# A gated DeltaNet layer on one core: inverse substitution in place, two batches in turns, a third vt buffer

## The chip, the cores and the metric

The kernel runs on one core of a Trainium2 chip. The metric is the device time of one execution, in microseconds. Engines are named as the profile names them: PE (matrix multiplications, with PEld for its weight loads), DVE (vector), ACT (activation), POOL and SP. SP computes nothing here; it issues most DMA transfers, and ACT and POOL issue the others.

## The reference

The reference is one layer of a diffusion backbone over 1024 latent tokens and 256 context tokens, with 1024 channels. A combined projection feeds two groups of four heads each: a gated DeltaNet that runs over the sequence in both directions, and a retention with rotary positions. Both are followed by norms and gates, one output projection, a SwiGLU and a final norm. What matters here is the gated DeltaNet, which inverts a unit triangular matrix for each chunk, head and direction:

```python
A = jnp.where(strict, jnp.einsum('nbhid,nbhjd->nbhij', kb, kc) * decay, 0.0)
rhs = jnp.concatenate([vc * bc[..., None], kb * jnp.exp(G)[..., None]], axis=-1)
sol = lax.linalg.triangular_solve(A + jnp.eye(CHUNK, dtype=A.dtype), rhs,
                                  left_side=True, lower=True, unit_diagonal=True)
```

The inverse does not depend on the state that the scan carries, so all chunks can be inverted before the scan over the chunks starts.

## The kernel before

The kernel works on ten chunks of 128 tokens, the first two of them context. For each chunk, head and direction there is one 128×128 triangular matrix, 80 in all. They are treated in three batches, `BATCH=[[0,1,2,9],[3,8,4,7],[5,6]]`, in the order in which the two scans need them: 32, 32 and 16 matrices.

**pre(t)** makes the matrices of a chunk. PE multiplies keys with keys into `kk` (line 705) and keys with queries into `kq` (line 715). SP loads a row of gate sums, broadcast, into `gw` (718); POOL masks it into `e` (722); ACT takes exponentials (726); DVE multiplies into `ut` (730) and `sp` (732). SP writes `ut` to `un` in DRAM, one tensor a batch (733), and `sp` into the scan's store `sd` (737).

**invert(b)** inverts the four 32×32 diagonal blocks of each matrix of a batch, one block a partition, so that batches 0 and 1 use 128 partitions and batch 2 uses 64. Four DMAs gather the blocks from `un` in DRAM into `yr` (751). The blocks of one direction are copied by ACT into `L` (758); those of the other are turned on the way by DVE (759). POOL sets `X` to the identity (755, 756). Then there are 31 steps of forward substitution, each a product on DVE (765) and a subtraction (767) that depends on it; the next step depends on that. A turned copy `XT` is made (769), and both are written to `xd` in DRAM (771).

**blocks(b)** and **merge(b)** make the 128×128 inverses from the blocks. SP loads the whole batch from `un` into `U` (783; 2 MB for batches 0 and 1), the diagonal blocks from `xd` over U's diagonal (787), and others into `t64` (788). PE then works in two levels: first `m` from `t64` and `U` (807), a negated copy `xt1` on DVE (810), and products of `xt1` with `U` (814, 817); then the same on blocks of 64 (830, `xt2` at 831, 834). The result goes to `sd`.

**The values.** For each of four heads `conv_block` projects and convolves the value head, with PE at lines 611 to 613, eight DVE operations at line 621 (in segments) and the SiLU on ACT at 624. PE turns the result into `vT` (856), in a PSUM bank that ACT empties into `vt` (859), and ACT issues the write to `sd` (860). `vt` has two buffers.

**token-major** matmuls `tm` (371 to 373) of the gates and the retention projections fill PE's time around the merges; there are 1248 in this phase. Their weights are split by ACT into `whi` (344) and by DVE or POOL into `wlo` (345). Afterwards the scan's steps load `pk` (664) and run `Tr`, `kS`, `up` and others (906 on).

The order of instructions on each engine isn't written out by hand. The program's text gives the dependences and the priorities, and a scheduler with a timeline of its own lays all instructions of the program out. A change in one place so moves instructions in other places too. Each engine, and each DMA queue behind an issuing engine, then runs its row in order: an instruction that waits holds up what stands behind it.

Of the kernel before, what the change touches and what calls it, by code (L numbers as in the profile page):

```python
# [8 lines left out]
F32 = mybir.dt.float32  # L9
F32R = mybir.dt.float32r  # L10
I32 = mybir.dt.int32
AF = mybir.ActivationFunctionType
# [13 lines left out]
H = 4  # L26
# [12 lines left out]
def build(nc, tc, ap, dbg=None, stop=None, marks=None):  # L39
# [151 lines left out]
    try:  # L191
# [508 lines left out]
        def pre(t):  # L700
# [15 lines left out]
            for d in range(2):  # L716
# [13 lines left out]
                V.tensor_tensor(ut.rearrange("p h i -> p (h i)"), pk, e.rearrange("p h i -> p (h i)"), ALU.mult)  # L730
# [12 lines left out]
        def invert(b):  # L743

            nc_ = len(BATCH[b])
            nu = nc_ * H
            nb = 4 * nu
            xd = xds[b] = dr.tile([4 * nb, 1024], F32, tag="xd%d" % b, name="xd%d" % b)
            yr = GI.tile([P, 1024], F32, tag="yr", name="yr", bufs=1)
            for k in range(4):  # L750
                SY.dma_start(yr[k:2 * nb:4].rearrange("r (i j) -> r i j", j=32),
                             un[b][q32[k]].rearrange("i e u j -> (e u) i j")[:, :, q32[k]])
            L = GI.tile([P, 1024], F32, tag="L", name="L", bufs=3)
            X = GI.tile([P, 1024], F32, tag="X", name="X", bufs=2)
            G.memset(X, 0.0)
            G.memset(X[:, 0::33], 1.0)
            m = lambda t: t[:2 * nb].rearrange("p (i j) -> p i j", j=32)
            S.activation(L[:nb], yr[:nb], AF.Copy)
            V.tensor_copy(m(L)[nb:], yr[nb:2 * nb].rearrange("p (i j) -> p j i", j=32))
            for j in range(31):  # L760
                n = 31 - j
                tmp = GI.tile([P, 256], F32, tag="tmp%d" % b, name="tmp", bufs=2)
                t3 = tmp[:2 * nb, :n * (j + 1)].rearrange("p (i c) -> p i c", c=j + 1)
                sh = [2 * nb, n, j + 1]
                V.tensor_tensor(t3, bc(m(L)[:, j + 1:, j], sh, 2), bc(m(X)[:, j, :j + 1], sh, 1), ALU.mult)
                xs = m(X)[:, j + 1:, :j + 1]
                V.tensor_tensor(xs, xs, t3, ALU.subtract)
            XT = GI.tile([P, 1024], F32, tag="L", name="XT", bufs=3)
            V.tensor_copy(m(XT), X[:2 * nb].rearrange("p (i j) -> p j i", j=32))
            for i, x in enumerate((X[:nb], XT[nb:2 * nb], X[nb:2 * nb], XT[:nb])):  # L770
                SY.dma_start(xd[i * nb:(i + 1) * nb], x)
# [20 lines left out]
        def merge(b):  # L792
# [17 lines left out]
            V.tensor_scalar(xt1.rearrange("p n j -> p (n j)")[:, :nu * 32], ps1[:, :nu * 32], -1.0, None, ALU.mult)  # L810
# [14 lines left out]
            for n0 in range(0, nu, 8):  # L825
# [5 lines left out]
                V.tensor_scalar(xt2.rearrange("p n j -> p (n j)"), ps1, -1.0, None, ALU.mult)  # L831
# [9 lines left out]
        def solve(b):  # L841
            for t in BATCH[b]:
                pre(t)
            checkpoint("pre%d" % b)
            invert(b)
            checkpoint("inv%d" % b)

        solve(0)
        solve(1)
        for h in range(H):  # L850
            y = newy()
            conv_block(8 + h, y, False)
            for t0, n in ((0, 2), (2, 4), (6, 4)):
                ps = bank_a("vT")
                for t in range(t0, t0 + n):
                    T.transpose(ps[:, (t - t0) * P:(t - t0 + 1) * P], y[:, t * P:(t + 1) * P], ident)
                vt = CV.tile([P, 4, P], F32, tag="vt", name="vt", bufs=2)
                for t in range(n):
                    S.activation(vt[:, t], ps[:, t * P:(t + 1) * P], AF.Copy, scale=sv3[:, t0 + t, h:h + 1])  # L859
                S.dma_start(vd[t0:t0 + n, :, h, :].rearrange("t p j -> p t j"), vt[:, :n])  # L860
# [12 lines left out]
        invert(2)  # L873
# [781 lines left out]
```

## Time and profile before

| | us |
|---|---|
| median of 3 runs | 1481.14 |
| lowest, highest | 1479.71, 1481.17 |
| the profiled execution's own time | 1477.96 |
| its span, first to last instruction | 1476.2 |
| PE busy in the span | 1397.2 |
| DVE busy | 964.6 |
| ACT busy | 614.0 |
| POOL busy | 590.3 |

The mean granted PE clock was 0.983. The profiled execution is one of its own; its times are read from the first instruction on. In the rows of a timeline stand start, length, engine, line, operation, and what it writes and reads; in square brackets the idle time of the engine before it and what ended that. PEq, SPq and the like are the sequencers that issue.

### The profile page before, as it was taken

The page shows a single profiled execution, that of the slowest core. Times are in us where ns is not written, and L with a number is a line of the kernel's source. Part 1 is how long each engine was busy: PE and PEld are TensorE (multiplying, and loading weights), DVE is VectorE, ACT ScalarE, POOL GpSimd, SP SyncE. Part 2 cuts the span into 40 slices and gives each one's busy share as a digit, 9 for nine tenths or more (in the row PEclk, how much of TensorE's full clock was granted, in tenths as well). Part 3 has the DMA queues.
Part 4 walks back from the last instruction along what each step waited for, and adds up shares of the span by engine and source line. Part 5 has one row for each costly group of instructions (what it writes and reads, how often), then busy time and mean ns, then how long its engine had stood idle before and what let it go on. Part 6 is the DMA issues. An engine that isn't in the chain of part 4 may idle for free.

```text
span 1476.2 us, 24111 instructions
## 1 busy us (share of the span) xinstructions
PE 1397.2 (95%) x8919; PEld 1199.2 (81%) x8919; DVE 964.6 (65%) x1856; ACT 614.0 (42%) x1326; POOL 590.3 (40%) x501
## 2 busy tenths in 40 slices
PE   7999999986789999899799899999999999999997
PEld 2898888975689999898688688877888888788885
DVE  6566789289792435689676877556555564657477
ACT  5643564587333111245443623233333332444445
POOL 0120010243202344234144688898555552335321
PEclk9999999998899999999899999999999999999999
DMA  9536686688888625996532265674222242776863
GB/s 337 197 105 205 189 249 200 219 264 277 282 216 277 238 76 178 416 341 209 184 125 104 97 238 210 242 264 162 105 97 105 107 151 79 260 260 194 288 216 114
DMA packets 170421, 298.14 MB, mean 202 GB/s; under 512 B 43496, under 2 KB 93880, under 8 KB 165952
## 3 DMA queue, kind: packets, MB, share of 16 engines
q1 hardware_dynamic: 118752, 253.17, 50.2%
q10 hardware_dynamic: 49072, 35.83, 7.8%
q0 software_dynamic: 2480, 7.60, 1.4%
q8 instruction: 70, 1.15, 0.3%
q14 instruction: 47, 0.39, 0.1%
HBM read 206.60 MB, written 89.96 MB: 201 GB/s over the span
## 4 chain that ended last, share of the span: by engine, by line
PE 55%; POOL 6%; DMA 5%; DVE 4%; issue 2%; ACT 2%; SPq 1%; ACTq 0%; POOLq 0%; DVEq 0%
PE ffn L1344 7%; PE ffn L1342 6%; PE ffn L1343 6%; PE fo L1470 4%; PE fo L1469 4%; PE fo L1468 4%; PE tm L371 3%; PE tm L373 3%; PE tm L372 3%; PE op L1203 2%; PE op L1201 2%; PE op L1202 2%; DMA wd<-tw 2%; POOL ws L1315 1%; DMA pk<-sd 1%
## 5 line engine op out<-in xcount | busy, mean ns | idle before, releaser
L371 PE MATMUL tm<-whi,hhi 128*128 128x256 f32 (+1 forms) x704 | 199.5, 287 | 7.7 <-ACT vt L859 3.4
L372 PE MATMUL tm<-wlo,hhi 128*128 128x256 f32 (+1 forms) x704 | 199.3, 285 | 2.4 <-issue 2.0
L373 PE MATMUL tm<-whi,hlo 128*128 128x256 f32 (+1 forms) x704 | 197.7, 285 | 0.0
L371 PEld LDWEIGHTS tm<-whi,hhi 128*128 128x128 f32 x704 | 132.8, 190 | 11.8 <-ACT vt L859 3.6
L1342 PE MATMUL ffn<-t,whi 128*128 128x512 f32 x352 | 136.9, 390 | 1.3 <-ACT whi L344 1.3
L1344 PE MATMUL ffn<-t,wlo 128*128 128x512 f32 x352 | 137.0, 390 | 1.0 <-DVE wlo L345 1.0
L1343 PE MATMUL ffn<-t,whi 128*128 128x512 f32 x352 | 137.0, 389 | 0.0
L372 PEld LDWEIGHTS tm<-wlo,hhi 128*128 128x128 f32 x704 | 133.7, 190 | 2.1 <-issue 0.9
L373 PEld LDWEIGHTS tm<-whi,hlo 128*128 128x128 f32 x704 | 132.8, 190 | 2.6 <-issue 1.8
L344 ACT ACTIVATE whi<-wraw 128x512 fp32r<-128x512 f32 (+2 forms) x98 | 75.1, 771 | 141.4 <-PE ffn L1343 80.5
L344 ACT ACTIVATE whi<-ws 128x512 fp32r<-128x512 f32 x88 | 55.6, 632 | 171.5 <-PE ffn L1343 123.4
L345 DVE TENSOR_TENSOR wlo<-ws,whi 128x512 fp32r<-128x512 f32 x88 | 93.9, 1068 | 47.0 <-ACT whi L344 46.8
L1469 PE MATMUL fo<-wlo,ahi 128*128 128x512 f32 x308 | 120.2, 390 | 2.1 <-DVE wlo L345 2.1
L1468 PE MATMUL fo<-whi,ahi 128*128 128x512 f32 x308 | 119.3, 390 | 0.7 <-ACT ahi L344 0.7
L1470 PE MATMUL fo<-whi,alo 128*128 128x512 f32 x308 | 119.0, 390 | 0.0
L345 DVE TENSOR_TENSOR wlo<-wraw,whi 128x512 fp32r<-128x512 f32 (+2 forms) x92 | 99.4, 1082 | 24.6 <-ACT whi L344 24.6
L1342 PE MATMUL ffn<-b,whi 128*128 128x512 f32 x264 | 103.8, 393 | 4.4 <-ACT whi L344 4.4
L1344 PE MATMUL ffn<-b,wlo 128*128 128x512 f32 x264 | 103.6, 393 | 0.8 <-DVE wlo L345 0.8
L1343 PE MATMUL ffn<-b,whi 128*128 128x512 f32 x264 | 103.4, 392 | 0.0
L612 PE MATMUL b<-hlo,whi 128*128 128x512 f32 (+1 forms) x256 | 94.4, 369 | 0.0
L613 PE MATMUL b<-hhi,wlo 128*128 128x512 f32 (+1 forms) x256 | 94.3, 368 | 0.0
L611 PE MATMUL b<-hhi,whi 128*128 128x512 f32 (+1 forms) x256 | 94.3, 368 | 0.0
(446 smaller groups left out, 3448.1 us busy)
## 6 DMA issues: line engine op xcount, KB each, us to landing
adaw<-ada SPq DMA_DIRECT2D x48, 512.0 KB, 4.4
pk<-sd SPq DMA_DIRECT2D x16, 1536.0 KB, 10.0
wraw<-wfi SPq DMA_DIRECT2D x44, 512.0 KB, 3.7
ar<-ad SPq DMA_DIRECT2D x33, 512.0 KB, 4.7
w<-wfo SPq DMA_DIRECT2D x22, 512.0 KB, 5.7
wd<-tw SPq DMA_DIRECT2D x11, 1024.0 KB, 4.8
ad<-act SPq DMA_DIRECT2D x20, 512.0 KB, 3.0
raw<-wd SPq DMA_DIRECT2D x20, 512.0 KB, 4.9
```

Source lines behind the costliest of these rows:

```text
L344: S.activation(hi, raw, AF.Copy)
L345: e.tensor_tensor(lo, raw, hi.bitcast(F32), ALU.subtract)
L371: T.matmul(o, hhi[:, k, tsl], whi[:, k % 4, :], start=(k == 0), stop=False)
L372: T.matmul(o, hhi[:, k, tsl], wlo[:, k % 4, :], start=False, stop=False)
L373: T.matmul(o, hlo[:, k, tsl], whi[:, k % 4, :], start=False, stop=(k == KT - 1))
L612: T.matmul(o, whi[:, k, :], hl, start=False, stop=False)
L1342: T.matmul(o, whi[:, k, :], xhi(xn, slice(0, 4), k), start=(first and k == 0), stop=False, **kw)
L1343: T.matmul(o, whi[:, k, :], xlo(xn, slice(0, 4), k), start=False, stop=False, **kw)
L1344: T.matmul(o, wlo[:, k, :], xhi(xn, slice(0, 4), k), start=False, stop=(k == 3), **kw)
L1468: T.matmul(po[g][i], ahi[:, ts], whi, start=(j == 0 and not kw), stop=False, **kw)
L1469: T.matmul(po[g][i], ahi[:, ts], wlo, start=False, stop=False, **kw)
L1470: T.matmul(po[g][i], alo[:, ts], whi, start=False, stop=(j == FH - 1), **kw)
```

## The change

`ut` is written negated. `invert` takes several batches at once. The blocks of the direction that need not be turned are gathered directly into `X`; the others go into `yr` (now two buffers) and are turned by DVE into `X`. There is no `L` any more, no POOL memset and no ACT copy: `X` starts as the negated matrix, its diagonal is set to one by a small DVE memset, and the steps replace its columns in place. Step 0 falls away, a step works on `j` columns rather than `j + 1`, and subtractions become additions. Where two batches are given, a step writes both products, then both additions. The four gathers of a batch become eight of half the size. `XT` takes its buffers from `X`'s tag. `xt1` and `xt2` become plain copies, and `vt` gets a third buffer.

The order of calls changes as well: `invert(0)` stands alone behind the first batch's `pre`, and `invert(1, 2)` stands behind `merge(0)` where `invert(2)` stood.

```diff
-                V.tensor_tensor(ut.rearrange("p h i -> p (h i)"), pk, e.rearrange("p h i -> p (h i)"), ALU.mult)
+                V.scalar_tensor_tensor(ut.rearrange("p h i -> p (h i)"), pk, -1.0, e.rearrange("p h i -> p (h i)"),
+                                       ALU.mult, ALU.mult)
...
-            for k in range(4):
-                SY.dma_start(yr[k:2 * nb:4].rearrange("r (i j) -> r i j", j=32),
-                             un[b][q32[k]].rearrange("i e u j -> (e u) i j")[:, :, q32[k]])
-            L = GI.tile([P, 1024], F32, tag="L", name="L", bufs=3)
-            X = GI.tile([P, 1024], F32, tag="X", name="X", bufs=2)
-            G.memset(X, 0.0)
-            G.memset(X[:, 0::33], 1.0)
-            m = lambda t: t[:2 * nb].rearrange("p (i j) -> p i j", j=32)
-            S.activation(L[:nb], yr[:nb], AF.Copy)
-            V.tensor_copy(m(L)[nb:], yr[nb:2 * nb].rearrange("p (i j) -> p j i", j=32))
-            for j in range(31):
+        def invert(*bs):
+
+            steps = []
+            for b in bs:
+                nb = 4 * len(BATCH[b]) * H
+                yr = GI.tile([P, 1024], F32, tag="yr", name="yr", bufs=2)
+                X = GI.tile([P, 1024], F32, tag="X", name="X", bufs=4)
+                for e, to in enumerate((X, yr)):
+                    for k in range(4):
+                        SY.dma_start(to[e * nb + k:(e + 1) * nb:4].rearrange("r (i j) -> r i j", j=32),
+                                     un[b][q32[k], e].rearrange("i u j -> u i j")[:, :, q32[k]])
+                m = lambda t, n=2 * nb: t[:n].rearrange("p (i j) -> p i j", j=32)
+                V.tensor_copy(m(X)[nb:], yr[nb:2 * nb].rearrange("p (i j) -> p j i", j=32))
+                V.memset(X[:2 * nb, 0::33], 1.0)
+                steps.append((b, nb, X, m))
+            for j in range(1, 31):
                 n = 31 - j
...
-                V.tensor_tensor(t3, bc(m(L)[:, j + 1:, j], sh, 2), bc(m(X)[:, j, :j + 1], sh, 1), ALU.mult)
-                xs = m(X)[:, j + 1:, :j + 1]
-                V.tensor_tensor(xs, xs, t3, ALU.subtract)
-            XT = GI.tile([P, 1024], F32, tag="L", name="XT", bufs=3)
...
+                for b, nb, X, m in steps:
...
+                    V.tensor_tensor(t3, bc(m(X)[:, j + 1:, j], sh, 2), bc(m(X)[:, j, :j], sh, 1), ALU.mult)
+                    part.append(t3)
+                for (b, nb, X, m), t3 in zip(steps, part):
+                    xs = m(X)[:, j + 1:, :j]
+                    V.tensor_tensor(xs, xs, t3, ALU.add)
...
-        solve(0)
-        solve(1)
+        for t in BATCH[0]:
+            pre(t)
+        invert(0)
+        for t in BATCH[1]:
+            pre(t)
...
-                vt = CV.tile([P, 4, P], F32, tag="vt", name="vt", bufs=2)
+                vt = CV.tile([P, 4, P], F32, tag="vt", name="vt", bufs=3)
...
-        invert(2)
+        invert(1, 2)
```

The layout moves instructions at two places of which the prediction speaks. The first is SP's row of DMA issues around merge 0. `X_4327` is batch 1's matrix in the kernel after, `X_4339` batch 2's; `yr_4440` is batch 2's gather before; `xd0` holds the inverted blocks of batch 0, `U0` and `t64_4177` or `t64_4064` are the tiles of merge 0, and `U1` is that of merge 1. Before:

```order
L783 DMA U1_4550<-un1_2893 128x4096
L771 DMA xd0_3079<-X_3086 64x1024 x2
L771 DMA xd0_3079<-XT_3184 64x1024 x2
L751 DMA yr_4440<-un2_2894 16x32x32 x3
L783 DMA U0_4175<-un0_2892 128x4096
L872 DMA rope_4049<-rope 128x1280
L751 DMA yr_4440<-un2_2894 16x32x32
L788 DMA t64_4177<-xd0_3079 32x32x32 x4
L787 DMA U0_4175<-xd0_3079 32x32x32 x4
```

Now:

```order
L776 DMA xd0_3181<-XT_3182 64x1024
L753 DMA X_4327<-un1_2893 16x32x32 x3
L788 DMA U0_4062<-un0_2892 128x4096
L873 DMA rope_3936<-rope 128x1280
L753 DMA X_4327<-un1_2893 16x32x32
L753 DMA X_4339<-un2_2894 8x32x32
L793 DMA t64_4064<-xd0_3181 32x32x32 x4
L753 DMA X_4339<-un2_2894 8x32x32 x3
L788 DMA U1_4544<-un1_2893 128x4096
L792 DMA U0_4062<-xd0_3181 32x32x32 x4
L776 DMA xd1_4530<-X_4327 64x1024 x2
```

U1's 2 MB load moved from ahead of inverse 0's writes to a place between merge 0's `t64` loads and its loads of U0's diagonal blocks, and batch 1's last direct gather stands behind U0's 2 MB.

The second place is DVE's row in the middle of inverses 1 and 2, where `tmp` is a product and `X<-X,tmp` the operation that depends on it; operations of 128 partitions belong to batch 1, those of 64 to batch 2. Before, batch 1 alone:

```order
L765 TENSOR_TENSOR tmp<-L,X 128x252
L767 TENSOR_TENSOR X<-X,tmp 128x18x14
L765 TENSOR_TENSOR tmp<-L,X 128x255
L767 TENSOR_TENSOR X<-X,tmp 128x17x15
L765 TENSOR_TENSOR tmp<-L,X 128x256
L767 TENSOR_TENSOR X<-X,tmp 128x16x16
```

Now, the two batches:

```order
L766 TENSOR_TENSOR tmp<-X 128x238
L766 TENSOR_TENSOR tmp<-X 64x184
L770 TENSOR_TENSOR X<-X,tmp 128x17x14
L770 TENSOR_TENSOR X<-X,tmp 64x23x8
L766 TENSOR_TENSOR tmp<-X 128x240
L766 TENSOR_TENSOR tmp<-X 64x198
L770 TENSOR_TENSOR X<-X,tmp 128x16x15
L770 TENSOR_TENSOR X<-X,tmp 64x22x9
```

An addition now has an operation of the other batch between itself and its product. Batch 2 lags seven steps behind and finishes alone.

More of the change, by code (lines that the diff above doesn't have):

```diff
@@ new lines, in invert @@
+        def invert(*bs):
[13 more added lines that the diff above has]
+            for j in range(1, 31):
+                n = 31 - j
+                part = []
+                for b, nb, X, m in steps:
+                    tmp = GI.tile([P, 240], F32, tag="tmp%d" % max(b, 1), name="tmp", bufs=2)
+                    t3 = tmp[:2 * nb, :n * j].rearrange("p (i c) -> p i c", c=j)
+                    sh = [2 * nb, n, j]
+                    V.tensor_tensor(t3, bc(m(X)[:, j + 1:, j], sh, 2), bc(m(X)[:, j, :j], sh, 1), ALU.mult)
[3 more added lines that the diff above has]
+                    V.tensor_tensor(xs, xs, t3, ALU.add)
+            for b, nb, X, m in steps:
+                xd = xds[b] = dr.tile([4 * nb, 1024], F32, tag="xd%d" % b, name="xd%d" % b)
+                XT = GI.tile([P, 1024], F32, tag="X", name="XT", bufs=4)
+                V.tensor_copy(m(XT), X[:2 * nb].rearrange("p (i j) -> p j i", j=32))
+                for i, x in enumerate((X[:nb], XT[nb:2 * nb], X[nb:2 * nb], XT[:nb])):
+                    SY.dma_start(xd[i * nb:(i + 1) * nb], x)
@@ L809, in merge @@
             xt1 = GM.tile([P, 16, 32], F32, tag="xt1", name="xt1", bufs=1)
-            V.tensor_scalar(xt1.rearrange("p n j -> p (n j)")[:, :nu * 32], ps1[:, :nu * 32], -1.0, None, ALU.mult)
+            V.tensor_copy(xt1.rearrange("p n j -> p (n j)")[:, :nu * 32], ps1[:, :nu * 32])
             ps2, ps3 = bank_b("m1"), bank_b("m1")
@@ L830, in merge @@
                         T.matmul(ps1[B, n * 64:n * 64 + 64], u[d][A, n0 + n, B], t[d][A, n0 + n, :], start=True, stop=True)
-                V.tensor_scalar(xt2.rearrange("p n j -> p (n j)"), ps1, -1.0, None, ALU.mult)
+                V.tensor_copy(xt2.rearrange("p n j -> p (n j)"), ps1)
                 for n in range(8):
@@ L839, in merge @@
             checkpoint("mrg%d" % b)
[L841 to L846, printed above, removed]
-        solve(0)
-        solve(1)
+        for t in BATCH[0]:
[3 more added lines that the diff above has]
+            pre(t)
         for h in range(H):
```

12 lines of the change are left out of this document (removed).

## The prediction

> **What bounds the kernel now.** The page comes first: the span, and the busy time of each engine.
>
> ```profile
> span 1476.2 us, 24111 instructions
> PE 1397.2 (95%) x8919; PEld 1199.2 (81%) x8919; DVE 964.6 (65%) x1856; ACT 614.0 (42%) x1326; POOL 590.3 (40%) x501
> ```
>
> PE leaves 1476.2 − 1397.2 = 79 us idle, and a change that takes no matmul away can only shorten that. So the windows come next, ten microseconds a row, the columns after the length being PE, PEld, DVE, ACT and POOL busy, PE clock, DMA share and GB/s:
>
> ```profile
> 350.00:360.00 10.00, 5.07 (x37) 4.46 (x36) 9.83 (x16) 9.68 (x20) 4.40 (x4) 0.90 0.78 223
> 360.00:370.00 10.00, 4.00 (x20) 3.61 (x20) 8.05 (x13) 5.48 (x25) 1.99 (x2) 0.67 0.93 302
> 370.00:380.00 10.00, 4.95 (x29) 4.95 (x30) 9.52 (x21) 6.74 (x18) 4.54 (x3) 0.58 0.76 265
> 380.00:390.00 10.00, 6.62 (x56) 6.41 (x55) 4.70 (x10) 2.85 (x7) 3.49 (x4) 1.00 0.92 312
> 400.00:410.00 10.00, 8.55 (x184) 7.92 (x183) 9.48 (x21) 2.77 (x4) 0.00 (x0) 1.00 1.03 194
> 410.00:420.00 10.00, 7.11 (x223) 6.80 (x222) 8.99 (x28) 5.25 (x9) 0.00 (x0) 0.83 0.72 209
> 550.00:560.00 10.00, 10.00 (x88) 10.00 (x87) 4.12 (x8) 3.20 (x4) 5.86 (x10) 1.00 0.48 165
> ```
>
> From 350 to 390 PE idles 4.93 + 6.00 + 5.05 + 3.38 = 19.4 us, while DVE is busy 9.8, 8.1 and 9.5 of ten in the first three rows; from 400 to 420 it idles 1.45 + 2.89 = 4.3. Later in the token-major phase it is full. PE's timeline names the waits (start, length, instruction, idle time before it and what ended it):
>
> ```profile
> 375.06 2.39 PE L856 MATMUL vT<-ident,y 128*128 128x128 f32 x10 [9.27 <-ACT y L624]
> 387.02 0.39 PE L371 MATMUL tm<-whi,hhi 128*128 128x256 f32 x1 [3.38 <-ACT vt L859]
> 406.15 0.39 PE L371 MATMUL tm<-whi,hhi 128*128 128x256 f32 x1 [1.35 <-ACT whi L344]
> 406.46 1.48 PE L807 MATMUL m<-t,U 32*32 32x32 f32 x124
> 411.85 0.22 PE L814 MATMUL m<-U,xt 32*32 32x32 f32 x2 [0.93 <-DMA U<-xd]
> ```
>
> Three places: A, the last value head's transposes, behind its convolution on DVE; B, a bank of PSUM that the last vt copy gives back late; C, merge 0, whose second step waits for U0's diagonal blocks.
>
> **A: DVE up to the last convolution.** Two waits stand there on ACT and DVE.
>
> ```profile
> 366.79 1.14 ACT L859 ACTIVATE vt<-vT,svy 128x128 f32<-128x128 f32 x4 [3.91 <-DMA sd<-vt]
> 369.74 0.69 DVE L730 TENSOR_TENSOR ut<-kk,e 128x512 f32<-128x512 f32 x1 [1.95 <-ACT e L726]
> 370.34 1.27 DVE L621 SCALAR_TENSOR_TENSOR y<-u,cw,y 128x1022 f32<-128x1022 f32 x1
> 318.44 2.47 DVE L765 TENSOR_TENSOR tmp<-L,X 128x112 f32<-128x112 f32 x1
> ```
>
> ACT stood 3.91 us for a vt buffer, the exponentials behind it came late, and DVE lost 1.95 us. A third buffer removes both. What is late next is the exponentials' own chain: the gw load, POOL's select. In the new order one gw load of this stretch stands behind batch 1's eight gathers on SP; in the old it stood behind four. DVE's work is not less here: by the order 37 inverse operations stand ahead of the last convolution, as before (7830 elements for 7893), since the step that is saved comes off the end. Some of them are stretched beside POOL's work (2.47 us for 112 columns at 318.44, where 255 columns take 0.42 below); POOL's memsets go, but which operations meet its larger ones is left open. I take −1.5, the smaller part of the two waits, with ends 0 and −3.
>
> **B: the bank.** The last two vt copies on ACT:
>
> ```profile
> 376.90 1.14 ACT L859 ACTIVATE vt<-vT,svy 128x128 f32<-128x128 f32 x4 [0.50 <-PE vT L856]
> 385.83 1.14 ACT L859 ACTIVATE vt<-vT,svy 128x128 f32<-128x128 f32 x4 [7.78 <-DMA sd<-vt]
> ```
>
> With three buffers the copy at 385.83 follows that at 376.90 at once, near 378.1, and the bank is back before PE asks for it at 387.02 − 3.38 = 383.6. This takes away 3.4 whole. What is then late is nothing of PE's: tm matmuls fill it up to merge 0.
>
> **C: merge 0 and SP's queue.** Rows of DVE and SP around the end of inverse 0, and the 2 MB loads' median time to landing:
>
> ```profile
> 381.01 2.20 DVE L769 COPY XT<-X 128x1024 f32<-128x1024 f32 x1
> 375.45 0.51 SPq L783 DMA_DIRECT2D U<-un  x1
> 383.24 4.87 SPq L771 DMA_DIRECT2D xd<-XT x2
> 391.78 0.56 SPq L783 DMA_DIRECT2D U<-un  x1
> 393.59 10.27 SPq L788 DMA_DIRECT2D t<-xd x4
> 403.89 3.41 SPq L787 DMA_DIRECT2D U<-xd x4
> U<-un SPq DMA_DIRECT2D x2, 2048.0 KB, 8.2
> ```
>
> Behind the last convolution there were 20 inverse operations, three of pre and XT; now there are 11 and three. From 370.34 + 1.27 to 383.21 were 11.6 us; nine operations of about 0.35 with their gaps (3.4) and XT's length (2.2 to 1.1 us) go, which leaves 6.5 to 7, and A's 1.5 comes on top: XT0 ends near 377.5. With xd's writes and three of batch 1's new gathers U0's load goes out at 382 to 386, say 383.5, 8.3 earlier than 391.78. The four t64 loads behind it then go the same 8.3 earlier.
>
> But the U0 diagonal blocks do not. In the old order U1's 2 MB went out at 375.45, long before. In the new it stands between t64's loads and U0's diagonal blocks. The old row shows what small gathers pay behind 2 MB: four t64 issues took 10.27 us behind U0, where the four U issues took 3.41. From U0's issue to the end of the t64 issues were 403.86 − 391.78 = 12.1 us, and the bulk of merge 0's first step could run at 406.46, 14.7 after it: t64 had landed 12 to 14.5 us behind U0's issue. The same behind U1: t64 done at 403.9 − 8.3 = 395.6, three gathers of inverse 2 (1.8), U1 out at 397.5, U0's blocks landed 12 to 14.5 later, at 409.5 to 412. PE, 1.5 + 3.4 = 4.9 us ahead, reaches them near 411.85 − 0.93 − 1.35 − 4.9 = 404.7 (both waits of C taken out) and stands there 5 to 7 us. Against 411.85 the place is reached at 410.3, so of A and B together only about 1.5 us is left here. Were the diagonal blocks not held up at all, the whole 4.9 and the 2.3 would be kept: ends 0 and −7.
>
> **Inverses 1 and 2.** Rows of the steps, alone and beside independent work:
>
> ```profile
> 389.32 0.20 DVE L765 TENSOR_TENSOR tmp<-L,X 128x31 f32<-128x31 f32 x1 [5.03 <-ACT L L758]
> 399.69 0.42 DVE L765 TENSOR_TENSOR tmp<-L,X 128x255 f32<-128x255 f32 x1
> 400.14 0.42 DVE L767 TENSOR_TENSOR X<-X,tmp 128x255 f32<-128x255 f32 x1
> 363.12 1.28 DVE L732 TENSOR_TENSOR sp<-kq,e 128x512 f32<-128x512 f32 x2
> 415.24 1.09 DVE L769 COPY XT<-X 128x1024 f32<-128x1024 f32 x1
> 441.89 1.12 DVE L769 COPY XT<-X 64x1024 f32<-64x1024 f32 x1
> ```
>
> A dependent step operation of 0.42 starts 0.45 after the last: 0.03 of gap. Two independent operations (the x2 row) take 1.28 together, where one such takes 0.68 or 0.69: 0.08 of overlap. So an operation in turns saves about 0.115 us, an estimate from these rows. By the order batch 1 goes alone to j = 7; its other 46 operations and as many of batch 2 stand in turns, say 94, and 94 × 0.115 = 10.8 us.
>
> Batch 1's steps start when its last direct gather has landed. That gather now stands behind U0: 383.5 + 8.2 and its own 1.3 = 393, against 389.32. The memset on DVE waits for it, and behind the memset stand all steps, the two wlo subtractions of the next weights and merge 0's xt1; 16 short steps later, near 398.5, the weights come, still ahead of PE's use, which was at 406.15.
>
> Old work from the first step: 441.89 + 1.12 − 389.32 = 53.7. New: less 10.8, less two operations of an inverse twice (4 × 0.2 = 0.8), less batch 2's copy, which now stands ahead of 393 (1.1, like the XT copies): 41.0. XT2 ends at 434, XT1 13 operations and a copy earlier, near 429, 13 later than 416.3.
>
> On SP batch 2's writes now stand ahead of batch 1's loads, so the first t64 piece is issued two writes behind XT2 (2 × 0.85, a quarter of 3.41 each) and lands 4.5 later (the four U loads were out by 407.3, and PE had the last at 411.85): 440.2. Merge 1 starts later in PE's order as well: 384 tm matmuls stand ahead of it, where there were 304. Those 80 extra are 80 × 0.118 = 9.4 us of PE work (390.07 and 390.18 are neighbouring starts):
>
> ```profile
> 390.07 0.28 PE L372 MATMUL tm<-wlo,hhi 128*128 128x256 f32 x1
> 390.18 0.28 PE L373 MATMUL tm<-whi,hlo 128*128 128x256 f32 x1
> 432.70 1.29 PE L807 MATMUL m<-t,U 32*32 32x32 f32 x128
> ```
>
> 432.70 − 1.5 + 9.4 = 440.6: half a microsecond of slack. The later pieces are asked for later too, with tm matmuls between in the order. I take 0, with ends 0 and +3.
>
> The rest is small. The negation in ut rides on an operation of the same size; xt1 and xt2 change form at the same size; both 0.
>
> **The scan.** The scan's third step now stands behind 840 of the phase's 1248 tm matmuls, where it stood behind 1058, and half a scan step more is done ahead of the last of them. With it SP sends eleven pk loads ahead of the loads of the next phase, where it sent ten. What PE waits for there is such a load:
>
> ```profile
> 591.43 15.38 DMA pk<-sd
> 606.86 1.86 PE kS L914 x8
> pk<-sd SPq DMA_DIRECT2D x8, 1536.0 KB, 11.8
> 590.00:600.00 10.00, 8.60 (x74) 8.22 (x74) 9.96 (x31) 2.41 (x5) 4.23 (x4) 1.00 1.04 419
> ```
>
> At 419 GB/s with the DMA engines full (share 1.04), 1.57 MB less is 3.7 us. I take −2, ends 0 and −4.
>
> **Sum.** C holds what A and B leave: −1.5; merge 1: 0; scan: −2; together −3.5 on the profiled execution of 1477.96 (span 1476.2 and 1.76 around it), that is 1474.4. The median of the runs shown is 3.18 above that execution, so 1477.6.
>
> **Rivals.** *U0's blocks are not held up* (0.20). If the transfers of U1 and of the gathers share the engines instead of standing in line, C keeps −7, and the scan gives −2: 1481.1 − 9 = 1472. For it: the four U issues took 3.41 with nothing large ahead. Against: the 10.27.
>
> *Turns save nothing on DVE, merge 1 waits* (0.25). This one is slower. Strided step operations of 0.42 may not overlap as the x2 rows do. Then XT2 ends 10.8 later, at 445, t64 lands at 451, PE comes at 440.6 and stands 10.4 us there: 1477.6 + 10.4 = 1488. The place is merge 1's first step; it decides against the forecast's gain once 3.9 of the 10.8 are lost, at a saving under 0.07 us an operation. For it: no row of before shows two step operations side by side. The Trainium skill (VectorE: DVE Perf Modes, section The DRAIN you can't avoid) speaks for it: the next operation starts only when the pipe has emptied, and eight copies took the same 13.88 us with a semaphore after each as with one. By that rule the sum is this rival's. Here the trace disagrees with it in part, since 1.28 is less than twice 0.68.
>
> *No change* (0.18). U0's blocks land at 412 and the scan's load is not earlier for being queued earlier, the engines being full: 0 to −1.5, 1480.5.
>
> **How the numbers follow.** The forecast has 0.34, its own range is 1475 to 1480; 0.03 is left for what isn't named. 0.2% of 1481.1 is 3 us, about what a measurement can tell: faster is below 1478.2. Faster: 0.20 + 0.27 of the forecast's 0.34 + 0.02; same: 0.07 + 0.16 + 0.01; slower: 0.25 + 0.02. The range from 1470 to 1488 takes in the rivals' times and leaves out the ends beyond.
>
> **What would show it.** A and B right: no wait for vt on PE or ACT, PE full from about 375 to merge 0. C right: a wait of 5 to 7 us of PE for U<-xd with U1's 2 MB ahead; if it is under 1, the first rival holds. Turns right: neighbouring step operations start about 0.34 apart; at 0.45 the second holds, with a wait of some 10 us at merge 1's first step. The scan right: the pk wait near 15 us is 2 to 4 shorter. I am wrong altogether if PE idles longer before 375, where a late gw load would show.

## The result, and the profile after

| | before | after |
|---|---|---|
| median, us | 1480.43 (4 runs, 1479.31 to 1481.17) | 1499.83 (4 runs, 1496.70 to 1503.03) |
| ratio | | 1.0131, interval 1.0111 to 1.0151 |
| profiled execution, us | 1477.96 | 1496.70 |
| its span, us | 1476.2 | 1494.9 |
| mean granted PE clock | 0.983 | 0.976 |

The change makes the kernel 19.4 us slower. The forecast was 1477.6, its range 1470 to 1488: wrong in sign and outside the range. The slower rival named a cost on DVE that is not there either.

First the page's busy times of the kernel after.

```profile
span 1494.9 us, 24107 instructions
PE 1404.6 (94%) x8919; PEld 1207.1 (81%) x8919; DVE 957.7 (64%) x1853; ACT 611.4 (41%) x1323; POOL 589.5 (39%) x495
```

PE is busy 7.4 us longer with the same 8919 matmuls. At half the granted clock a tm matmul starts 0.213 us after the last one, and at the full clock 0.118 (last section), so its busy time grows and this is a sign of the clock; the windows show where (columns as in the prediction).

```profile
370.00:380.00 10.00, 5.02 (x22) 4.73 (x23) 9.69 (x20) 8.97 (x29) 4.32 (x3) 0.50 0.76 265
380.00:390.00 10.00, 10.00 (x79) 10.00 (x79) 3.07 (x3) 1.86 (x7) 3.56 (x2) 0.90 0.94 280
400.00:410.00 10.00, 7.81 (x167) 7.22 (x166) 6.39 (x21) 2.77 (x4) 0.00 (x0) 0.83 0.96 224
410.00:420.00 10.00, 2.24 (x22) 1.93 (x21) 10.00 (x38) 0.69 (x2) 0.00 (x0) 0.80 1.15 263
420.00:430.00 10.00, 8.12 (x231) 7.81 (x232) 6.42 (x21) 3.91 (x7) 0.00 (x0) 0.51 0.12 35
450.00:460.00 10.00, 6.00 (x38) 5.55 (x38) 2.45 (x2) 3.08 (x5) 0.00 (x0) 0.85 1.20 186
470.00:480.00 10.00, 7.54 (x118) 7.15 (x104) 0.99 (x4) 3.42 (x6) 1.03 (x3) 0.66 0.38 123
```

From 380 to 390 PE is full where it idled 3.38. From 400 to 430 it idles 2.19 + 7.76 + 1.88, and the clock is 0.51 in the last of these rows, where that of before was full at clock 1.00. Holes follow at 450 and 470. Read in windows of 1 us from 390 to 500, PE's idle time rises from 7.8 to 19.4 and the busy time lost to the clock (busy times one minus the clock) from 1.7 to 9.7: 11.6 + 8.0 = 19.6 us, against 18.7 by which the span grew. So in the trace the loss stands at merge 0 and merge 1. From 290 to 390 the same sum falls by 1.2 only; from 500 to 880 it rises by 2.5.

PE's timeline names the waits.

```profile
374.19 2.08 PE L715 MATMUL kq<-qc,kc 128*128 128x128 f32 x8 [5.82 <-ACT qt L712]
377.06 2.40 PE L857 MATMUL vT<-ident,y 128*128 128x128 f32 x10 [0.79 <-ACT y L624]
402.67 0.28 PE L812 MATMUL m<-t,U 32*32 32x32 f32 x2 [2.19 <-DMA t<-xd]
418.26 0.23 PE L819 MATMUL m<-U,xt 32*32 32x32 f32 x1 [6.34 <-DVE tmp L766]
420.91 1.75 PE L822 MATMUL m<-xt,U 32*32 32x32 f32 x57 [2.33 <-DMA U<-xd]
454.55 0.21 PE L812 MATMUL m<-t,U 32*32 32x32 f32 x2 [2.54 <-issue]
456.54 0.24 PE L812 MATMUL m<-t,U 32*32 32x32 f32 x2 [1.46 <-DMA t<-xd]
```

The wait of 6.34 is put down to a step operation on DVE, but its neighbour 2.6 us later waits for U0's diagonal blocks, and so does this one by its operands: xt1 was copied at 410.62. SP's timeline shows why they come late.

```profile
382.49 0.53 SPq L776 DMA_DIRECT2D xd<-X  x1
387.71 2.96 SPq L753 DMA_DIRECT2D X<-un  x3
390.77 0.55 SPq L788 DMA_DIRECT2D U<-un  x1
391.89 1.29 SPq L753 DMA_DIRECT2D X<-un  x2
393.29 9.22 SPq L793 DMA_DIRECT2D t<-xd  x4
404.74 0.47 SPq L788 DMA_DIRECT2D U<-un  x1
405.32 10.93 SPq L792 DMA_DIRECT2D U<-xd  x4
449.62 0.43 SPq L792 DMA_DIRECT2D U<-xd  x1
```

U0's 2 MB go out at 390.77, only 1.0 earlier than before. The small gathers behind them take 9.22, and those behind U1's 2 MB 10.93. Merge 1's first small load goes out at 449.62, since the matrices that it reads were late. DVE's rows show that.

```profile
379.79 1.09 DVE L774 COPY XT<-X 128x1024 f32<-128x1024 f32 x1
402.18 0.09 DVE L757 MEMSET X<- 128x32 f32 x1 [19.04 <-DMA t<-xd]
419.88 0.69 DVE L766 TENSOR_TENSOR tmp<-X 128x238 f32<-128x238 f32 x2
420.49 0.69 DVE L770 TENSOR_TENSOR X<-X,tmp 128x238 f32<-128x238 f32 x2
439.70 1.12 DVE L774 COPY XT<-X 128x1024 f32<-128x1024 f32 x1
444.12 1.12 DVE L774 COPY XT<-X 64x1024 f32<-64x1024 f32 x1
```

DVE stands 19.04 us until batch 1's matrix is there. The view names t<-xd, but the memset writes X, and by its operand it waits for X's last direct gather, which was issued at 391.89, behind U0's 2 MB; in no_turns and warm, two kernels of the next section with that gather behind U0 too, the view does name X<-un. Inverse 1 began at 389.32 before. In turns, a pair of step operations starts every 0.61 us.

### The profile page after: what moved, and what is told of

It is laid out like the page before. It is cut to its first block, busy times and chain, and to the rows that moved or that the text cites. A ratio compares the mean times of both kernels' runs of the same rounds, so it can differ in the third digit from the quotient of the medians.

```text
span 1494.9 us, 24107 instructions
## 1 busy us (share of the span) xinstructions
PE 1404.6 (94%) x8919; PEld 1207.1 (81%) x8919; DVE 957.7 (64%) x1853; ACT 611.4 (41%) x1323; POOL 589.5 (39%) x495
## 5 line engine op out<-in xcount | busy, mean ns | idle before, releaser
L371 PE MATMUL tm<-whi,hhi 128*128 128x256 f32 (+1 forms) x704 | 202.8, 291 | 3.0 <-ACT xa L384 1.9
```

The source lines that it names most:

```text
L371: T.matmul(o, hhi[:, k, tsl], whi[:, k % 4, :], start=(k == 0), stop=False)
```

## The experiments

Each ratio is to the kernel before on the same chip.

| kernel | what it is | median, us | ratio, interval |
|---|---|---|---|
| after | | 1499.83 | 1.0131 (1.0111 to 1.0151) |
| vt3 | before, third vt buffer | 1487.08 | 1.0058 (1.0038 to 1.0078) |
| vt3_rope | the same, rope load by POOL | 1491.24 | 1.0071 (1.0043 to 1.0099) |
| u1_pool | after, U1's 2 MB by POOL | 1492.92 | 1.0088 (1.0065 to 1.0111) |
| no_turns | after, inverses 1 and 2 one by one | 1492.92 | 1.0091 (1.0069 to 1.0113) |
| old_place | after, inverses where they stood | 1492.52 | 1.0089 (1.0066 to 1.0112) |
| after_vt2 | after, two vt buffers | 1506.58 | 1.0184 (1.0167 to 1.0201) |
| sub_only | old_place, two vt buffers | 1501.61 | 1.0153 (1.0121 to 1.0185) |
| warm | after, PE kept busy at merge 0 | 1491.46 | 1.0076 (1.0052 to 1.0100) |
| old_load | sub_only, blocks loaded as before | 1479.33 | 1.0003 (0.9985 to 1.0021) |
| halves_only | before, halves loaded directly | 1500.62 | 1.0140 (1.0121 to 1.0159) |
| x_pool | after, X's direct gathers by POOL | 1490.84 | 1.0076 (1.0055 to 1.0097) |
| after_old_load | after, blocks loaded as before | 1484.70 | 1.0036 (1.0018 to 1.0054) |
| direct0 | old_load, batch 0 direct | 1488.61 | 1.0059 (1.0038 to 1.0079) |
| direct1 | old_load, batch 1 direct | 1481.49 | 1.0010 (0.9997 to 1.0023) |
| direct2 | old_load, batch 2 direct | 1484.15 | 1.0034 (1.0019 to 1.0050) |
| turns_vt2 | old_load with the turns | 1484.76 | 1.0041 (1.0020 to 1.0061) |
| after_d0 | after, only batch 0 direct | 1483.83 | 1.0042 (1.0023 to 1.0061) |
| after_d12 | after, only batches 1 and 2 direct | 1491.55 | 1.0101 (1.0061 to 1.0140) |

### First round: which part

After the result there were four theories. HELD: the loss is merge 0's blocks held up behind SP's queue and U1's 2 MB, the mechanism of the prediction at a greater price. PLACE: the loss comes of where the calls of `invert` now stand. TURNS: the turns bring it, since batch 1 ends with batch 2. VT: the third buffer alone sets off the new layout.

**vt3.** `bufs=2` to `bufs=3` for vt in the kernel before, nothing else.

> The kernel before with the third vt buffer alone. If the buffer is worth what the prediction took for bank wait B, PE's 3.38 us in front of the tm matmul at 387 go, nothing else gets worse, and the time is 1474 to 1479 us against 1480.4. If any new layout of the program costs time by itself, however small the edit, it is 1481 or more.

It lost 7.8 us by the median. From 290 to 390 the idle and clock time falls by 3.3 us, of the 4.9 that A and B foresaw together; from 390 to 500 it rises from 9.5 to 22.7. In its layout U1's and U0's 2 MB go out together ahead of xd0's writes, and PE waits for a bank at 397.20:

```profile
397.20 0.39 PE L371 MATMUL tm<-whi,hhi 128*128 128x256 f32 x1 [3.74 <-ACT res L532]
```

**u1_pool.** The 2 MB of U1 are issued by POOL.

```diff
-            SY.dma_start(uu.rearrange("p e c h j -> p e (c h) j"), un[b])
+            (G if b == 1 else SY).dma_start(uu.rearrange("p e c h j -> p e (c h) j"), un[b])
```

> The changed kernel, but the 2 MB load of U1 is issued by POOL, where its place is ahead of inverse 0's end, and SP's row no longer has it in front of U0's diagonal blocks. Theory HELD (the loss is U0's diagonal blocks behind U1's 2 MB, with what follows from it: the idle DVE, the late merge 1, the lower PE clock): PE's waits at merge 0's second step (6.3 and 2.3 us) fall under 1, and the time is 1482 to 1489 us. Theory PLACE (the loss is that batch 1 is inverted behind merge 0, together with batch 2, so that merge 1 comes too late whatever the loads do): the time stays at 1494 or more.

PE's waits at merge 0's second step are gone, as HELD said, but the time lies between the two ranges: 7 us of 19 come back. So U1's place can have a part, but not the whole. Inverse 1 starts later still here, with a wait of 24.39 us for X<-un on DVE.

**no_turns** writes `invert(1); invert(2)` for `invert(1, 2)`; **old_place** puts `invert(1)` behind the `pre` of its batch and `invert(2)` behind `merge(0)`, as before the change.

> The changed kernel with inverse 1 and inverse 2 one after the other in the place where they now stand in turns. Theory HELD: the layout still has U1's 2 MB ahead of U0's diagonal blocks (even ahead of t64), so merge 0 waits 8 us or more and the time is 1496 to 1505 us. Theory TURNS (writing batch 1's blocks only behind batch 2's steps is what makes merge 1 late): batch 1's blocks are out some 8 us earlier, and the time is 1485 to 1492.

> The changed kernel with inverse 1 back behind the second batch's pre, as before, and inverse 2 behind merge 0: only the new substitution, the direct halves and the third vt buffer are left of the change. The layout still has U1's 2 MB ahead of U0's diagonal blocks, though behind t64. Theory HELD: a wait of 5 us or more for U<-xd at merge 0 and 1484 to 1495 us. Theory PLACE: batch 1 is ready early, and the time is 1474 to 1481.

Each gains 7 and keeps 13. old_place lies in HELD's range, with waits of 6.52 and 2.42 us for U<-xd; no_turns lies between its two ranges. The two kernels, which differ in the place of inverse 1, take the same time. The turns cost something and the places do not make up the rest: neither PLACE nor TURNS holds alone.

### Second round: the buffer, the rope load, the clock

**after_vt2** and **sub_only** take the third buffer away, from after and from old_place. By VT the loss goes with it.

> The changed kernel with two vt buffers as before; all else of the change stays. In this layout U1's 2 MB stands ahead of batch 0's xd writes again, as in the kernel before, and nothing large stands between t64's loads and U0's diagonal blocks. Theory VT (the third buffer is what costs: with it the vt copies and their DMA issues pass ahead of the qt squares on ACT, and the large loads fall to worse places on SP): 1478 to 1486 us, and PE's waits at merge 0's second step under 2 us. Rival PLACE (batch 1's inverse behind merge 0, in turns, is what costs): 1490 or more, with merge 1 as late as in the changed kernel.

> Only the new substitution with its direct halves, on the old places of the inverses and with two vt buffers. Theory VT: 1475 to 1483 us, against 1492.5 for the same with three buffers. If the substitution itself costs (eight gathers a batch for four, DVE's small memset behind them), 1486 or more.

VT is refuted: without the buffer both are slower, by 6.8 and 9.1 us. sub_only has the inverses in their old places, so PLACE does not explain its 22 us either; what is left in it is the substitution with its direct halves. The same buffer cost 7.8 in the kernel before. Its sign depends on the layout around it.

**vt3_rope** lets POOL issue the rope load in vt3, which stood in SP's row ahead of xd0's writes.

> The kernel before with the third vt buffer, and the load of the rope table issued by POOL, so that SP's row no longer stands still behind its wait (from 380.7 to 396.4 us in the run with the third buffer alone) ahead of batch 0's xd writes. If that wait is what the third buffer costs, merge 0 comes some 10 us earlier and the time is 1476 to 1481; if the 4 MB of U1 and U0 that go out together ahead of the xd writes are what costs, it stays at 1484 to 1488.

Nothing is gained, and the time lies even above the 1484 to 1488; the 4 MB that go out together remain as the likelier cause in vt3, which was not tried further.

**warm** adds 60 matmuls 128×128 of xt1 with itself into merge 0's result bank ahead of its second step, which overwrites them: work that PE is to do while it would idle.

```diff
+            if b == 0:
+                xf = xt1.rearrange("p n j -> p (n j)")
+                for _ in range(60):
+                    T.matmul(ps2[:, :P], xf[:, :P], xf[:, :P], start=True, stop=True)
```

> The changed kernel with sixty matmuls more (128 by 128, from xt1, written to a bank that the second step of merge 0 then overwrites) in PE's row between xt1 and that step, where PE otherwise waits some 6 us for U0's diagonal blocks. Theory CLOCK (each idle stretch also costs half the PE clock for the next few us): the granted clock stays at 1.0 from 412 to 421 or so and the time is 2 to 5 us shorter than the changed kernel's, 1495 to 1498, though PE has more to do. If the clock is no part of the loss, the time is that of the changed kernel or up to 7 us longer.

With 13.56 us more of matmuls the kernel is 8.4 us faster by the median. A window of 1 us in after (the clock is the third number from the end):

```profile
422.00:423.00 1.00, 1.00 (x69) 1.00 (x67) 1.00 (x5) 0.08 (x1) 0.00 (x0) 0.50 0.09 16
```

The same window in warm, with the added matmuls (L820) and the second step behind them (L823):

```profile
422.00:423.00 1.00, 1.00 (x12) 1.00 (x11) 1.00 (x5) 0.00 (x0) 0.00 (x0) 1.00 0.22 50
413.27 13.56 PE L820 MATMUL m<-xt 128*128 128x128 f32 x120
426.76 0.21 PE L823 MATMUL m<-U,xt 32*32 32x32 f32 x1
```

In after the clock is halved from 416 to 429 and the second step and the first tm behind it run at it, as the row of 420 to 430 above shows; in warm it stays at 1.00 from 408 to 448. CLOCK's condition is met, and the time falls by more than the 2 to 5 us that it named, but the gain does not stand at merge 0. The second step comes at 426.76, later than in after (418.26 and 420.91). From 390 to 500 idle and clock time is 16.4 us, and with the 13.56 of added work that makes 30.0, where after has 29.1. warm's profiled execution is only 2.3 us shorter than after's, and from 500 to 680 the sum is 3.8 for 8.6. So this run does not show that the half clock at merge 0 costs time that a warm PE would save: the added work takes as long as it spares, and the layout moved with it.

### Third round: how the blocks are loaded

HALVES: it is the direct loading, eight half-size gathers a batch for four. **old_load** takes sub_only and loads as before:

```diff
-                for e, to in enumerate((X, yr)):
-                    for k in range(4):
-                        SY.dma_start(to[e * nb + k:(e + 1) * nb:4].rearrange("r (i j) -> r i j", j=32),
-                                     un[b][q32[k], e].rearrange("i u j -> u i j")[:, :, q32[k]])
+                for k in range(4):
+                    SY.dma_start(yr[k:2 * nb:4].rearrange("r (i j) -> r i j", j=32),
+                                 un[b][q32[k]].rearrange("i e u j -> (e u) i j")[:, :, q32[k]])
...
+                S.activation(X[:nb], yr[:nb], AF.Copy)
```

**halves_only** is the reverse: the kernel before, whose `L` gets its half by four gathers of its own and no ACT copy. **after_old_load** is old_load's edit in after, with turns and third buffer; **x_pool** lets POOL issue X's direct gathers in after.

> As the run with only the new substitution (old places, two vt buffers), but the blocks are loaded as before: four gathers of both halves into yr, then ACT's copy and DVE's turned copy into X. Theory HALVES (batch 1's direct gathers stand between batch 0's xd writes and U0's load, in a stretch where the DMA engines are full, and so hold up merge 0 and all behind it): with them gone SP's row around merge 0 is that of the kernel before, and the time is 1475 to 1484 us, against 1501.6. Rival LAYOUT (the kernel before has one good layout, and whatever is moved loses ten microseconds or more between 390 and 500): 1488 or more.

> The kernel before with the direct halves alone: L's untouched half is gathered straight from DRAM with four DMAs, the turned half goes through yr with four, ACT's copy falls away; old substitution, two vt buffers. Theory HALVES: 1490 to 1503 us, with merge 0's first matmuls some 6 us or more later than at 404. If it is the new substitution that costs, and not how its halves are loaded: 1478 to 1484.

> The changed kernel (batches 1 and 2 in turns behind merge 0, three vt buffers) with the blocks loaded as before: four gathers into yr, ACT's copy, DVE's turned copy. In this layout U1 and U0 go out together ahead of batch 0's xd writes, as in the run with the third buffer alone. Theory HALVES: better than the changed kernel by 5 us or more, 1484 to 1494. Rival LAYOUT: 1494 or more, since that order of loads cost 7.8 us by itself.

> The changed kernel with X's direct gathers issued by POOL, so that none stands on SP between batch 0's xd writes and U0's load. Theory HALVES as far as it is SP's row: U0's load goes out some 5 us earlier, and the time falls below 1495. If it is the DMA engines' own load in that stretch and not the row, the time stays at 1496 to 1503.

HALVES is right, in both directions. The substitution in place costs nothing (1.0003), and the direct halves alone bring 20.4 us into the kernel before. In after, loading as before takes 14 to 15 of the 19.4 away. x_pool gains 8 to 9 us, as HALVES said for SP's row: its two 2 MB loads go out at 386.48 and 388.94. SP's timeline of old_load, for the same stretch:

```profile
378.57 3.95 SPq L752 DMA_DIRECT2D yr<-un  x4
382.62 0.60 SPq L788 DMA_DIRECT2D U<-un  x1
386.39 0.53 SPq L788 DMA_DIRECT2D U<-un  x1
394.93 9.20 SPq L793 DMA_DIRECT2D t<-xd  x4
404.24 3.37 SPq L792 DMA_DIRECT2D U<-xd  x4
```

Batch 1's four gathers go out ahead of everything, both 2 MB loads follow, and the last of merge 0's blocks is issued by 407.6, against 416.3 in after. One caution about the sums by stretch: from 390 to 500 old_load has 17.4 us of idle and clock time where before has 9.5, and yet the times are equal. Such a sum says where a trace loses time, and part of it can be made up elsewhere (3.2 us from 290 to 390 here, 1.4 from 500 to 680).

### Fourth round: which halves

Around merge 0 two things differ in after's layout: U1's load stands ahead of U0's diagonal blocks (U1 theory), and batch 1's direct gathers stand behind xd0's writes (GATHER theory). COUNT says that each batch's extra gathers cost alike. **direct0**, **direct1**, **direct2** load one batch directly in old_load, by a condition on `b` around the two forms of the diff above. **turns_vt2** is old_load with `invert(1, 2)` behind `merge(0)`.

> The kernel old_load (substitution in place, two vt buffers, old places, all blocks gathered by four DMAs into yr), with the direct halves for batch 0 alone. old_load took 1479.3, with all three batches direct it was 1501.6. By the order, U1's 2 MB load now stands between merge 0's t64 loads and U0's diagonal blocks, but no gather of batch 1 stands ahead of U0's load. U1 theory (what costs is U1's place ahead of U0's diagonal): 1488 to 1502, with a wait of PE for U<-xd of 5 us or more and half clock behind it. GATHER theory (what costs is batch 1's direct gathers ahead of U0's load): 1477 to 1485. COUNT theory (each batch's extra gathers cost a third, wherever they stand): 1484 to 1490.

> The kernel old_load with the direct halves for batch 1 alone. By the order, batch 1's four direct gathers stand between batch 0's xd writes and U0's load, and U1's load between the t64 loads and U0's diagonal blocks: both suspects are there. U1 theory: 1488 to 1502. GATHER theory: 1490 to 1502. COUNT theory: 1484 to 1490.

> The kernel old_load with the direct halves for batch 2 alone. By the order, SP's row around merge 0 is that of old_load, with U1's load early; batch 2's direct gathers stand between batch 1's xd writes and merge 1's loads. U1 theory and GATHER theory: 1477 to 1485, for merge 0 is as in old_load, and batch 2's gathers can cost merge 1 some 2 to 4 us at most. COUNT theory: 1484 to 1490.

> The kernel old_load with batches 1 and 2 in turns, their call behind merge 0, and nothing else: all blocks gathered by four DMAs, two vt buffers. The same with three vt buffers took 1484.7, and old_load 1479.3. If the turns themselves gain where nothing holds up merge 0: 1470 to 1478, below both kernels. If DVE's time around the merges is hidden behind PE's tm matmuls anyway, 1478 to 1481. If the turns hold back merge 1, since batch 1 now ends with batch 2: 1482 to 1490, with PE waiting 2 us or more for t<-xd at merge 1.

U1 and GATHER theory both fall in the form they had: direct1 has both orders and loses 1 us. Its SP row:

```profile
384.61 4.14 SPq L753 DMA_DIRECT2D X<-un  x4
388.86 0.55 SPq L793 DMA_DIRECT2D U<-un  x1
389.52 9.47 SPq L798 DMA_DIRECT2D t<-xd  x4
399.72 0.43 SPq L793 DMA_DIRECT2D U<-un  x1
400.26 11.89 SPq L797 DMA_DIRECT2D U<-xd  x4
```

U0's diagonal blocks pay 11.89 behind U1, as in after, but the last is issued by 412.2 and PE has tm matmuls up to 416.25: no wait for them. And batch 1's gathers all stand ahead of U0's load, so inverse 1 starts at 390.87. The order alone costs nothing here; that the time at which these transfers go out decides is read from the traces, and no run changes it alone. sub_only says the same from the other side: there U1 goes out early, at 383.75, and 22 us are lost. direct0's loss stands elsewhere: its last vT comes at 384.50, 7.8 later than old_load's 376.71, and from 290 to 390 its idle and clock time is 33.7 us for 24.7, while its waits for U<-xd are under 2 us each. direct2's 4.8 us against old_load show in no stretch from 290 to 880. No count of gathers gives these three numbers, so COUNT falls too.

turns_vt2 is 5.4 us slower than old_load, though its inverse 2 ends 22 us earlier (XT2 at 419.8 for 442.4) and no wait of 0.7 us or more for t<-xd stands at merge 1. With no_turns (−6.9 from after) that is the second pair in which the kernel with the turns is 5 to 7 us slower. The second pair is not clean, since the call of inverse 1 moves behind merge 0 with the turns; in after that place made no difference (old_place and no_turns). Where the turns' time lies isn't settled: up to 500 the two kernels idle alike within 2 us, and from 500 to 680 turns_vt2 has some 4 us more, among them a wait for DVE in the scan:

```profile
664.39 0.84 PE L923 MATMUL Tr<-r,pk 128*128 128x128 f32 x4 [1.98 <-DVE r L918]
```

**after_d0** and **after_d12** make the same split in after itself.

> The kernel after with the direct halves for batch 0 alone; batches 1 and 2 by four gathers into yr and ACT's copy, as before. after took 1499.8, the same with all blocks loaded as before 1484.7. By the order no gather stands between xd0's writes and merge 0's loads, and U1 goes out right ahead of U0. If the loss comes from batch 1's and 2's direct gathers at merge 0: 1480 to 1488. If it comes from batch 0's, through the time of the values (as in direct0, where the last vT was 8 us late): 1491 to 1500. If only the three together bring it: 1480 to 1488 here and in after_d12 as well.

> The kernel after with the direct halves for batches 1 and 2 alone; batch 0 by four gathers and ACT's copy. By the order U1 goes out before xd0's writes, as in the kernel before, but all eight direct gathers of batches 1 and 2 stand between U0's load and t64's loads. If those gathers at merge 0 bring the loss: 1493 to 1502, with a wait of PE for t<-xd of 5 us or more. If U1's place ahead of U0's diagonal is needed for it, or batch 0's halves: 1480 to 1490.

Batch 0's halves cost nothing clear of noise in after (1.0042 against after_old_load's 1.0036). Those of batches 1 and 2 bring 9.6 us by the ratios, 1.0101 to 1.0036; the time lies between the two ranges expected, and the wait for t<-xd is there. DVE's rows of after_d0 first, then those of after_d12 and its wait at merge 1:

```profile
381.74 0.09 DVE L762 MEMSET X<- 128x32 f32 x1 [0.57 <-ACT X L759]
414.35 1.06 DVE L779 COPY XT<-X 128x1024 f32<-128x1024 f32 x1
```

```profile
403.03 0.09 DVE L762 MEMSET X<- 128x32 f32 x1 [16.51 <-DMA X<-un]
438.33 1.10 DVE L779 COPY XT<-X 128x1024 f32<-128x1024 f32 x1
```

```profile
456.63 0.28 PE L817 MATMUL m<-t,U 32*32 32x32 f32 x2 [5.21 <-DMA t<-xd]
```

In after_d12 all eight direct gathers stand behind U0's 2 MB. Inverse 1 starts 21 us later than in after_d0, its XT ends 24 later, and merge 1 waits 5.21. This is what after has too (402.18, 440.82). The rest of after's loss, 4.4 us between 1.0101 and 1.0131, appears when batch 0 is direct as well and U1's load moves behind the t64 loads; the intervals overlap, so it isn't separated.

Over all kernels one number goes with the time: the end of XT1. It lies between 410 and 423 in all that lose 0.6% or less, and between 424 and 446 in all that lose 0.7% or more. It is a companion and not the only cause: in x_pool inverse 1 could start at 386.46, XT1 still ended at 443.8, and 8 to 9 us were gained. Nor does it order the slower kernels among themselves: sub_only, at 1.5%, has 427.9.

None of them beat the kernel before; old_load and direct1 tie with it.

## Why the prediction was wrong, point by point

The step that failed is the clock time of U0's load, 390.77 for 383.5, and with it the 0 that was taken for inverse 1 and merge 1. The points follow in the prediction's order.

**A (−1.5) gave nothing.** The vt wait of 3.91 on ACT and the 1.95 on DVE went, but the last vT came at 377.06 for 375.06. DVE waited elsewhere instead, 1.16 + 1.38 for 1.95. These are its only waits of 330 to 374 in after:

```profile
339.18 0.69 DVE L730 SCALAR_TENSOR_TENSOR ut<-kk,e 128x512 f32<-128x512 f32 x1 [1.16 <-POOL sp L737]
362.09 0.69 DVE L730 SCALAR_TENSOR_TENSOR ut<-kk,e 128x512 f32<-128x512 f32 x1 [1.38 <-issue]
372.07 1.27 DVE L621 SCALAR_TENSOR_TENSOR y<-u,cw,y 128x1022 f32<-128x1022 f32 x1
```

The last convolution operation ended at 373.34 for 371.61, and the last y followed it. ACT's timeline shows who now pays for the free buffer:

```profile
366.80 2.42 ACTq L861 DMA_DIRECT2D sd<-vt  x2
369.27 0.26 ACT L712 ACTIVATE qt<-qt 128x128 f32<-128x128 f32 x1 [2.24 <-issue]
375.73 1.27 ACT L624 ACTIVATE y<-y 128x1280 f32<-128x1280 f32 x1
```

The vt copies and their DMA issues stand ahead of the query squares (712), the issues hold ACT for 2.24, and kq (715) on PE waits 5.82 for squares. The prediction followed ACT's row to DVE alone, not to PE. vt3 does not show A either: its 3.3 us less from 290 to 390 are about B's 3.4, and its last vT comes at 375.79, no earlier than before.

**B (−3.4) was right.** The two last vt copies follow one another (377.78 and 378.91 on ACT), and PE is full from 380 to 390.

**C was the right mechanism at the wrong time.** "The U0 diagonal blocks do not" come earlier, since U1's 2 MB stand ahead: so it is, and their four issues took 10.93 where the four of before took 3.41. But the sum took U0's issue at 383.5, and it was 390.77. XT0 ended at 380.88 for 377.5: A's 1.5 was missing, and two step operations, at 374.08 and 375.20, were stretched to 1.08 and 1.35 beside POOL's products for sp (373.75 to 376.40), the meeting that the prediction had left open. SP then needed 9.9 us from there to U0's load, where 6 were taken: 1.6 until the first write, behind two sd<-sp issues that end at 382.39, 5.2 for the four writes, 3.0 for the three new gathers. All else is this shift of 7.3: U1 at 404.74 for 397.5, and from there 16.2 us for 12 to 14.5 until the last blocks were in PE's reach at 420.91. PE waited 6.34 + 2.33 where 5 to 7 had been expected, and 9 us later than the 412 at which the sum still broke even. C's ends were 0 and −7: neither of them was a loss, though everything in C hung on one time.

**Inverse 1 was to start at 393 and started at 402.28.** Again 7.3 of U0's issue, and 11.4 from there to the memset where 9.5 were taken. The "half a microsecond of slack" at merge 1 was then used up many times: XT1 at 440.82 for 429, XT2 at 445.24 for 434, merge 1's first wait at 454.55. The prediction set the direct gathers down as a later start of DVE alone, worth 0. after_d12, with these gathers direct and batch 0's not, loses 9.6 us by them, the largest part that any run sets apart; that they act through the late start is argued from its rows.

**The turns on DVE were right, and worth nothing.** A pair every 0.61 is 0.305 an operation, where 0.34 was taken and 0.45 is a dependent one's. From the first step to XT2's end were 43.0 us for 41.0 predicted. So the slower rival is refuted by its own row: it wanted 0.45. The Trainium skill (VectorE: DVE Perf Modes, section The DRAIN you can't avoid), on which it leaned, says that the next operation starts only when the pipe has emptied, but also that a next operation that is not held starts earlier, which the rival left out. For operations that don't depend on each other this trace agrees with the second: the pair at 419.88 ends at 420.57, and the next starts at 420.49. But DVE's speed gained no time: turns_vt2 has the shorter inverses and is slower.

**The scan (−2) can't be read alone.** The pk wait of 1.12 on PE is gone, and the windows of 590 to 600 have a DMA share of 0.18 for 1.04, yet the last kS comes at 681.90 for 669.73, and idle and clock time from 680 to 880 is 25.6 us for 24.5. Nothing was gained there.

**The clock was missing from the sum.** All waits were priced at their length. Of the 19.6 us between 390 and 500 8.0 are counted as busy time at half clock; no run shows what they are worth alone.

**What is shown, and what is open.** Shown: the direct halves bring 14 to 15 of the 19.4 us and the turns 6 to 7, measured by undoing each in after (undone one by one the parts need not add up); the substitution in place brings none; the third buffer costs 7.8, gains 7 to 9 or does nothing according to the layout. Argued from traces: the way by the late start of inverse 1 and the blocks behind U1. Open: why the layout puts the direct gathers behind U0's load when all their data are there, 4.4 us of the halves, where the turns lose, and where warm gains.

## What to carry to other kernels

A change that spares one engine work but doubles the small transfers on a full queue is priced by the place of these transfers: four gathers of 128-byte rows behind a 2 MB load took 9 to 12 us to issue here in most layouts, and what starts from them moves with them. Where an automatic layout decides the order, test each part of a change alone in both directions: the same third buffer had all three signs. A sum whose margin is 0.5 us of slack needs the case in which the event ahead of it is 7 us late, for that delay reaches every later term at once.

## What the runs showed of the hardware that was not expected

**The clock halves after short waits, and the length of the wait alone doesn't say when.** In after a gap of 2.19 us, right behind a full stretch, halved it; in the kernel before a gap of 3.38 did not, and in vt3 one of 3.74 did (0.50 from 398 to 400). First after, then before, the window of 1 us behind the gap:

```profile
403.00:404.00 1.00, 1.00 (x5) 1.00 (x6) 0.88 (x4) 0.00 (x0) 0.00 (x0) 0.50 0.99 141
```

```profile
388.00:389.00 1.00, 1.00 (x11) 1.00 (x10) 0.00 (x0) 0.78 (x1) 0.64 (x2) 1.00 1.06 313
```

The half clock then lasted some 3 us, while a tm matmul started every 0.213 us and not every 0.118. The Trainium skill (TensorE: Matmul & The Clock Gate, section What's actually happening) tells of a gate to half clock after at least one idle window of about 3.4 us, with windows that run free. The half clock and the spread agree; that an idle stretch of 2.19 us is enough does not.

**Small gathers behind a large load.** Merge 0's four small loads of one kind (t<-xd or U<-xd) took 3.1 to 3.4 us to issue with nothing large right ahead (before, old_load, sub_only), and 9.2 to 11.9 as the first four of their kind behind a 2 MB load, in before, after, old_load, sub_only, halves_only and direct1. It is not a price on each: of U0's four in after one took 7.83 and the others about 1.0, and the two smaller gathers into X right behind U0's 2 MB (64 and 32 KB for 128) took 1.29 together. Nor is it fixed: direct2 has 6.39, and no_turns and after_d0, with two 2 MB loads ahead, 14.93 and 15.29. For one load the price was in the prediction, and it held in after; what was wrong was the clock time to which it was added.
